# q and k of three attention heads projected early and parked in DRAM, with the order of TensorE and VectorE written out beside the top-k selection

## The chip, the cores and the metric

The kernel runs on one core of one Trainium2 chip. The metric is the device time of one execution in microseconds, as the median of the runs shown. The engines are called by their profile names: PE (TensorE matmul), PEld (its weight loads), DVE (VectorE), ACT (ScalarE), POOL (GpSimd) and SP (SyncE, which issues most transfers).

## The reference, cut to what matters

One transformer block over 1024 positions of width 1024, all in float32: a modulation vector, a sparse attention whose 256 keys per query are picked by an index score, a gated linear attention (GLA), a mix of the two, and a gated feed-forward part.

```python
mod = silu(c) @ w_mod + b_mod                 # six vectors: sh1, sc1, g1, sh2, sc2, g2
h = rms_norm(x, norm1_g) * (1 + sc1) + sh1
q, k, v, q_idx, k_idx, w_idx, gq, gk, gv, go, g_lr = split(h @ w_in)
score = einsum(relu(q_idx . k_idx), w_idx * idx_scale), causal      # 8 index heads of 64
sel = top_k(score, 256)                       # per query
att = softmax(q . k[sel] * att_scale) @ v[sel]                      # 4 heads of 128
gla = gla_chunked(gq, gk, gv, log_sigmoid(g_lr @ w_gate2 + b_gate2) / 16)   # 4 heads, dk 64, dv 128
mix = concat(rms_norm(att), rms_norm(gla) * silu(go)) @ w_out
x = x + g1 * mix
h2 = rms_norm(x, norm2_g) * (1 + sc2) + sh2
x = x + g2 * ((silu(gate) * up) @ w_down);  out = rms_norm(x, final_g)
```

## The kernel before

Every large product splits both factors into a rounded part and a rest and takes three matmuls for one (hi*hi, lo*hi, hi*lo). One projection of a 128-wide weight (`proj_T_plain`, `qk_proj`) runs as two units of 24 matmuls of 512 columns, a T unit each (lines L239 to L241). One of a 256-wide weight (`proj_N_plain`) runs as eight units of 24 matmuls of 256 columns, an N unit each (L248 to L250).

The work goes through these stages. First x is normed and transposed and the index projections are made; `scores(t)` then makes the index scores of query tiles 2 to 7 (PE L535 and L536, ACT L538, DVE L543). After that `units(jobs, ...)` walks a list of projection jobs: q, k and v of the two GLA pairs, the gates (`go`), v of the attention, and last q and k of the four attention heads. It is a generator with one step per unit, and each step is followed by `pump()`, which advances the background generators by the rates of `RATE`. These are `topk_act` ("ta": a bitwise search for the 256th score of tiles 7, 6 and 5, with three Sign passes per bit on ACT, L619, and four small operations on DVE, L621 to L626), `topk_dve` ("td": the same search for tiles 4, 3 and 2 with three counting passes on DVE, L590), and `gla_pair` (seven levels with POOL, ACT, DVE work in `prep` and eight PE matmuls in `level`, L757, whose result DVE takes with L762, and then eight chunks, L806 to L814). The loop ends when q and k of head 0 have begun and drains the selection.

The attention loop takes heads 0 to 3 and tiles 0 to 7. `att_step` makes the scores of one tile (L913 to L915), the transposes of the tile before (L930) and the values of the one before that (L939). Between these steps the remaining T units of q and k of heads 1 to 3 run (`next(main)`), `mods_late` makes the modulation vectors 2 to 5 (loads of `w_mod` on SP, DVE L657 and L659), and in head 3 `side` makes the GLA half of the mix (`mix_mm(t, 1, ...)`, L1011 to L1013). What is left of `side` runs behind the attention; then come the attention half of the mix, the second norm, the gate and up products (L1175 to L1177) and the down product (L1353 to L1355).

The Tile framework collects the instructions in the order in which they are traced, and orders each engine's queue itself by priority and readiness; `tc.high_priority` moves instructions forward in that order. Each engine then works through its own queue in order. Tiles of one tag share `bufs` slots, and a new tile waits for a free slot: `g` has 33 slots of 4 KB per partition, `gs` 4, `raw` 2, and the rings `whi` and `wlo` 4 each.

Of the kernel before, what the change touches and what calls it, by code (L numbers as in the profile page):

```python
# [41 lines left out]

RATE = {"ta": (0.8, 0), "td": (0.83, 2), "gla0": (1.1, 0), "gla1": (1.12, 0),
        "mods": (1.74, 0), "side": (0.41, -2)}
PRIORITY = {"td": 40, "side": 150, "mods": -40}
PROJ_FIRST = (1, 0, 1, 0, 1, 0, 1, 0)
PROJ = 0.5

# [4 lines left out]
W0_AT = 3  # L53
G1_AT = 2
OFF_BIAS = 1.0e30
# [10 lines left out]
def hymba_block_kernel(  # L66
# [32 lines left out]
    x1_d = dram.tile([L, D], F32, name="x1_d")  # L99
    hid_d = dram.tile([DFF, L], F32, name="hid_d")  # L100
    uid = [0]

# [224 lines left out]
    def proj_T_plain(w, dst, scale=None):  # L327
        for hf in range(2):
            pt = ps()
            chain_T(pt, w, slice(0, 128), *hT(hf), slice(0, 512))  # L330
            r = slice(hf * 512, hf * 512 + 512)
            if scale is None:
                A.copy(dst[:, r], pt)
            else:
                A.mul(dst[:, r], pt, scale)
            yield

# [9 lines left out]

    def pump():

        for name in list(bg):  # L350
            it, rate, due = bg[name]
            due += rate
            while due >= 1:
                due -= 1
                with tc.high_priority(PRIORITY[name]) if name in PRIORITY else nullcontext():
                    end = next(it, "end") == "end"
                if end:
                    del bg[name]
                    break
            else:  # L360
                bg[name] = (it, rate, due)
# [6 lines left out]
    def gate(p, w):  # L368
        drain(f"gla{p}")
        yield from gate_proj(p, w)  # L370

# [21 lines left out]
    def qk_proj(h, i, w):  # L393
        hi, lo = g([P, L], F32R), g([P, L], F32R)
        qk[h, i] = (hi, lo)
        for hf in range(2):
            pt = ps()
            chain_T(pt, w, slice(0, 128), *hT(hf), slice(0, 512))
            r = slice(hf * 512, hf * 512 + 512)
            A.copy(hi[:, r], pt)  # L400
            V.tensor_tensor(lo[:, r], pt, hi[:, r].bitcast(F32), ALU.subtract)
            yield

# [17 lines left out]
    for kind, p in (("go", 0), ("v", 0), ("v", 1), ("go", 1)):  # L421
        c0, fn = (C_GO, gate) if kind == "go" else (C_V, v_proj)
        le, he = low(len(jobs)), high(len(jobs))
        jobs.append((lambda c0=c0, p=p, le=le, he=he: wgroup256(w_in, c0 + p * 256, le, he), lambda w, fn=fn, p=p: fn(p, w)))
    for h in range(ATT_H):
        for i in range(2):
            jobs.append(job_qk(h, i))

# [117 lines left out]

    bias = {t: score[t].bitcast(BF16)[:, :(t + 1) * P] for t in score}
    bias[0], bias[1] = bias01[:, P:], bias01
    junk_d = cst.tile([P, 640], BF16, name="junk_d")
    top = {4: sc3[:, 512:832], 2: sc3[:, 832:1024], 3: sc5[:, 768:1024]}  # L550
    top = {t: top[t].bitcast(BF16) for t in top}
# [24 lines left out]
    def topk_dve(ts):  # L576
# [9 lines left out]
        for i in range(32):  # L586
# [10 lines left out]
            else:  # L597
                V.tensor_tensor(Z, m[:, :n], Z, ALU.bitwise_xor)
            yield
        for j, t in enumerate(ts):  # L600
            finish(t, Z[:, j:j + 1].bitcast(F32))
            yield

    def topk_act(ts):
# [9 lines left out]
        for i in range(32):  # L614
# [12 lines left out]
            else:  # L627
                V.tensor_tensor(Y, m[:, :n], Y, ALU.bitwise_xor)
            yield
        V.tensor_scalar(Y, Y, -2147483648, None, ALU.bitwise_xor)  # L630
        V.tensor_scalar(F, F, -2147483648, None, ALU.bitwise_xor)
# [14 lines left out]

    def mods_late():
        def acc_of(m, n):
            acc = g([P, 512], tag="h", bufs=4)
            for i in range(4):  # L650
                raw = g([P, 2, 512], tag="raw", bufs=NRAW)
                S.dma_start(raw, w_mod[2 * i * P:2 * (i + 1) * P, m * D + n * 512:m * D + (n + 1) * 512]
                            .rearrange("(k p) n -> p k n", p=P))
                for j in range(2):
                    cc = cs[:, 2 * i + j:2 * i + j + 1]
                    if i == 0 and j == 0:
                        V.tensor_scalar(acc, raw[:, j, :], cc, None, ALU.mult)  # L657
                    else:
                        V.scalar_tensor_tensor(acc, raw[:, j, :], cc, acc, ALU.mult, ALU.add)  # L659
                yield  # L660
            return acc

        def summed(m, n, acc):
            pt = ps()
            if m in (2, 5):
                T.matmul(pt[0:1, :], lhsT=ones[:, 0:1], rhs=acc, start=True, stop=True)
                row = g([1, 512], tag="h", bufs=4)
                A.copy(row, pt[0:1, :])
# [12 lines left out]

        last = None
        for m in (2, 3, 4, 5):
            for n in range(2):
                acc = yield from acc_of(m, n)
                if last is not None:
                    summed(*last)
                last = (m, n, acc)
        yield
        summed(*last)  # L690

# [139 lines left out]
    def gate_proj(p, w):  # L831
# [5 lines left out]
        for t in range(NT):  # L837
# [5 lines left out]
            if t % 4 == 3:  # L843
                S.dma_start(gla_d[(t - 3) * P:(t + 1) * P, p * 256:(p + 1) * 256].rearrange("(a p) d -> p a d", p=P),
                            sg[t // 4])
            yield

# [46 lines left out]
    bg["td"] = (topk_dve(SEL_D), *RATE["td"])  # L894
    while len(qk) < 2:
        next(main)
        pump()
    next(main)
    for name in list(bg):
# [6 lines left out]
    def att_scores(h, t):  # L906
# [10 lines left out]
        mx = small(1, tag="mx")  # L917
        V.tensor_tensor_reduce(sb[:, :W], pt[:, :W], bias[t], 1.0, NEG, ALU.add, ALU.max, mx)
        V.tensor_scalar(mx, mx, -att_scale, None, ALU.mult)
        z = small(1, tag="z")  # L920
        A.activation(sb[:, :W], sb[:, :W], AF.Exp, bias=mx, scale=att_scale, accum_out=z)
        return sb, z
# [12 lines left out]
    def att_values(h, t, pT, z):  # L935
# [5 lines left out]
        V.reciprocal(z, z)  # L941
        V.tensor_scalar(att[h // 2][t // 4][:, t % 4, hv], po[:, :P], z, None, ALU.mult)

# [81 lines left out]
    def side():  # L1025

        nxt = gla_pre(0)
        for t in range(NT):
            cur, nxt = nxt, gla_pre(t + 1) if t + 1 < NT else None
            mix_mm(t, 1, *cur)  # L1030
            if t % 2:
                wout_chunk(t // 2)
            yield

    bg["mods"] = (mods_late(), *RATE["mods"])
    proj = 0
    for h in range(ATT_H):
        if h % 2 == 0:
            att[h // 2] = [g([P, 4, 256]) for _ in range(2)]
        if h == G1_AT:  # L1040
            g1b = mod_bcast(0, 2 * D)
        if h == 3:
            for _ in main:
                pass
            drain("mods")
            for k in range(4, 8):
                wout_chunk(k)
            bg["side"] = (side(), *RATE["side"])
        for t in range(NT):
            att_step((h, t))  # L1050
            proj += PROJ if h else PROJ_FIRST[t]
            while proj >= 1:
                proj -= 1
                next(main, None)
            pump()
# [230 lines left out]
    for name in ("t3", "22", "t2", "t4"):  # L1286
        for _ in range(2):
            prepare()
        for qq, cols in late:
            row_sums((name,), qq, cols)  # L1290
    for s, k in order:
        if k == 0 and not s.up:
            sg = [g([P, L]) for _ in range(2)]
# [10 lines left out]


    g2b = mod_bcast(1, 5 * D)
    fin, acc = {}, {}
# [105 lines left out]
```

## Time and profile before

| what | value |
|---|---|
| median of 3 runs | 1442.97 us (1439.71 to 1443.05) |
| the profiled execution's own time | 1440.6 us |
| its span, first to last instruction | 1438.9 us |
| mean granted PE clock | 0.954 |
| busy: PE, PEld, DVE, ACT, POOL | 93%, 78%, 63%, 40%, 29% of the span |

The span is 1.7 us shorter than the execution's own time, and that time lies 2.4 us under the median. A busy share is an average over stages with different limits, and matmuls overlap, so the time of a PE matmul in the profile is its latency and not the distance to the next one. The granted clock is told as a share of full speed: 1.00 is 2.4 GHz and 0.50 is 1.2 GHz.

### The profile page before, as it was taken

What the parts mean: (1) busy time and instruction counts of PE and PEld (TensorE: products, weight loads), DVE (VectorE), ACT (ScalarE), POOL (GpSimd) and SP (SyncE); (2) the same over time, 40 slices, a digit from 0 to 9 for tenths busy, and PEclk for the clock granted to TensorE, in tenths of its full rate; (3) what the DMA queues carried; (4) which work ended last, traced back from release to release, by engine and by line L of the source; (5) the groups of instructions that cost most, each with busy time, mean ns of one, the idle gap of its engine ahead of it and who ended that gap; (6) DMA issues with size and microseconds to landing.
All of it is one profiled execution on the core that took longest, in us unless ns stands there. A gap on an engine that the chain in (4) does not pass through costs nothing.

```text
span 1438.9 us, 18354 instructions
## 1 busy us (share of the span) xinstructions
PE 1337.6 (93%) x6975; PEld 1121.2 (78%) x6975; DVE 899.8 (63%) x1577; ACT 571.7 (40%) x1026; POOL 423.7 (29%) x365
## 2 busy tenths in 40 slices
PE   5999946888899999999997999999999999999997
PEld 4777846677789888788886788888888887888886
DVE  3578999988737657665369644544444546575524
ACT  3466544665554233363176323233332335112202
POOL 3550621165100000023122334444433525223101
PEclk8999978999679999999999999999999999999999
DMA  9601001101001526552031222221222346264102
GB/s 266 200 15 44 16 0 30 30 13 47 30 17 44 177 74 186 179 215 78 30 136 40 88 88 76 86 83 66 86 88 79 97 146 212 100 201 146 45 15 103
DMA packets 93438, 132.16 MB, mean 92 GB/s; under 512 B 6211, under 2 KB 67746, under 8 KB 93350
## 3 DMA queue, kind: packets, MB, share of 16 engines
q1 hardware_dynamic: 93192, 130.93, 28.6%
q8 instruction: 55, 0.90, 0.3%
q14 instruction: 33, 0.27, 0.1%
q10 hardware_dynamic: 158, 0.06, 0.0%
HBM read 108.94 MB, written 22.03 MB: 91 GB/s over the span
## 4 chain that ended last, share of the span: by engine, by line
PE 64%; DVE 19%; DMA 5%; issue 4%; ACT 3%; SPq 2%; POOL 2%; ACTq 0%; DVEq 0%; POOLq 0%
PE pw L1175 4%; PE pw L1176 4%; PE pw L1177 4%; PE ps L1177 4%; PE ps L1175 4%; PE ps L1176 4%; DVE junk_d L590 4%; PE pw L1353 3%; PE ps L1353 3%; PE pw L1355 3%; PE ps L1355 3%; PE pw L1354 3%; PE ps L1354 3%; DMA raw<-in_w_mod_dram 2%; DVE h L745 2%
## 5 line engine op out<-in xcount | busy, mean ns | idle before, releaser
L619 ACT ACTIVATE junk_a<-g,Ya 128x1024 int8<-128x1024 f32 (+2 forms) x96 | 99.8, 1039 | 93.8 <-DVE Ya L626 92.8
L248 PE MATMUL ps<-whi,g 128*128 128x256 f32 x384 | 114.6, 298 | 0.0
L249 PE MATMUL ps<-whi,g 128*128 128x256 f32 x384 | 113.1, 294 | 0.0
L250 PE MATMUL ps<-wlo,g 128*128 128x256 f32 x384 | 113.0, 294 | 0.0
L1206 POOL TENSOR_TENSOR g<-g,h 128x512 f32<-128x512 f32 x33 | 51.9, 1572 | 138.0 <-DVE h L1218 74.1
L1319 POOL TENSOR_TENSOR raw<-raw,g 128x1024 f32<-128x1024 f32 x22 | 58.7, 2676 | 110.0 <-DMA raw<-in_w_down_dram 103.2
L239 PE MATMUL ps<-g,whi 128*128 128x512 f32 x208 | 84.1, 404 | 0.0
L241 PE MATMUL ps<-g,wlo 128*128 128x512 f32 x208 | 82.6, 397 | 0.0
L240 PE MATMUL ps<-g,whi 128*128 128x512 f32 x208 | 82.2, 395 | 0.0
L1177 PE MATMUL ps<-g,wlo 128*128 128x512 f32 x192 | 75.6, 394 | 6.3 <-DVE wlo L1168 6.2
L248 PEld LDWEIGHTS ps<-whi,g 128*128 128x128 f32 x384 | 78.1, 203 | 1.6 <-issue 1.4
L1175 PE MATMUL pw<-g,whi 128*128 128x512 f32 x192 | 76.9, 400 | 1.5 <-DVE h L1224 1.5
L249 PEld LDWEIGHTS ps<-whi,g 128*128 128x128 f32 x384 | 78.1, 203 | 0.0
L250 PEld LDWEIGHTS ps<-wlo,g 128*128 128x128 f32 x384 | 77.7, 202 | 0.2 <-issue 0.2
L1175 PE MATMUL ps<-g,wlo 128*128 128x512 f32 x192 | 75.4, 393 | 0.7 <-ACT g L1080 0.7
L1176 PE MATMUL ps<-g,wlo 128*128 128x512 f32 x192 | 75.3, 392 | 0.4 <-DVE g L1081 0.4
L1176 PE MATMUL pw<-g,whi 128*128 128x512 f32 x192 | 74.9, 390 | 0.0
L1177 PE MATMUL pw<-g,whi 128*128 128x512 f32 x192 | 74.8, 390 | 0.0
L956 POOL TENSOR_TENSOR raw<-raw,g 128x1024 f32<-128x1024 f32 x4 | 9.6, 2388 | 214.3 <-DMA raw<-in_w_out_dram 214.3
L590 DVE TENSOR_SCALAR_CACHE_REDUCE junk_d<-g,Zd 128x640 bf16<-128x640 f32 (+5 forms) x96 | 71.4, 744 | 1.8
L1168 DVE TENSOR_TENSOR whi<-gs,whi 128x512 fp32r<-128x512 f32 x44 | 37.8, 858 | 45.3 <-ACT whi L1167 44.7
L757 PE MATMUL pw<-h,gs 128*128 128x128 f32 x224 | 34.9, 316 | 30.5 <-DVE ma L622 16.4
(394 smaller groups left out, 3884.6 us busy)
## 6 DMA issues: line engine op xcount, KB each, us to landing
raw<-in_w_gate_up_dram SPq DMA_DIRECT2D x42, 512.0 KB, 3.5
raw<-in_w_mod_dram SPq DMA_DIRECT2D x32, 512.0 KB, 3.6
raw<-in_w_in_dram SPq DMA_DIRECT2D x24, 512.0 KB, 3.5
hid_d<-g SPq DMA_DIRECT2D x22, 512.0 KB, 3.0
raw<-in_w_down_dram SPq DMA_DIRECT2D x22, 512.0 KB, 3.4
gs<-hid_d SPq DMA_DIRECT2D x22, 512.0 KB, 3.3
g<-in_x_dram SPq DMA_DIRECT2D x16, 512.0 KB, 6.1
g<-in_w_mod_dram SPq DMA_DIRECT2D x16, 512.0 KB, 8.7
```

Of the source, the lines that this page charges most:

```text
L239: T.matmul(pt, lhsT=wh, rhs=rh, start=(k == 0), stop=False)
L248: T.matmul(pt, lhsT=rh, rhs=wh, start=(k == 0), stop=False)
L249: T.matmul(pt, lhsT=rl, rhs=wh, start=False, stop=False)
L250: T.matmul(pt, lhsT=rh, rhs=wl, start=False, stop=(k == KC - 1))
L590: V.tensor_scalar(junk_d[:, :W], top[t] if 0 < i < 16 else score[t], Z[:, j:j + 1].bitcast(F32), -float(TOPK), ALU.is_ge, ALU.add, accum_o ...
L619: A.activation(junk_a[:, :W], score[t], AF.Sign, bias=Y[:, j:j + 1].bitcast(F32), accum_out=acc[:, j:j + 1])
L1175: T.matmul(pt, lhsT=w[:, 0, kk, :], rhs=rh, start=(not more and kk == 0), stop=False, skip_group_check=more)
L1176: T.matmul(pt, lhsT=w[:, 0, kk, :], rhs=rl, start=False, stop=False, skip_group_check=more)
L1177: T.matmul(pt, lhsT=w[:, 1, kk, :], rhs=rh, start=False, stop=(kk == 3), skip_group_check=more)
L1353: T.matmul(po[m], lhsT=ah[:, r], rhs=wh[:, cc], start=(f == 0), stop=False)
L1354: T.matmul(po[m], lhsT=al[:, r], rhs=wh[:, cc], start=False, stop=False)
L1355: T.matmul(po[m], lhsT=ah[:, r], rhs=wl[:, cc], start=False, stop=(f == len(cur) - 1))
```

## The change

The projections of q and k of heads 1 to 3 become jobs among the GLA, gate and value jobs (`PARK_AT`). Each writes its result as float32 into a `g` tile, and SP stores it to the DRAM tile `qk_d`. In the attention, `qk_load(h)` reads both back one head ahead and splits them again into two parts. The rates are lower, a T unit counts as 1.87 steps and a step of the gate as 0.3. All units, q and k of head 0 included, now run before the attention, and `pin()` ties every PE and every DVE instruction of that loop to the one traced before it on the same engine, so that the order of both queues is the traced one. The selection writes its masks to tiles of its own (`bias_tiles`), not over the scores. The modulation vectors are spread: vector 2 during the last gate job, 3 and 4 during the attention, with loads issued by POOL into slots of the ring `whi`, and 5 in the feed-forward stage (`mod_g2`). `side` begins at head 0. The row maximum takes its scale in the reduction itself, which saves one small DVE operation (L919) per tile, and the division by the softmax sum (L942) moves from DVE to ACT.

```diff
-RATE = {"ta": (0.8, 0), "td": (0.83, 2), "gla0": (1.1, 0), "gla1": (1.12, 0),
-        "mods": (1.74, 0), "side": (0.41, -2)}
-PRIORITY = {"td": 40, "side": 150, "mods": -40}
-PROJ_FIRST = (1, 0, 1, 0, 1, 0, 1, 0)
-PROJ = 0.5
+RATE = {"ta": (0.46, 0), "td": (0.46, 1), "gla0": (0.58, 0), "gla1": (0.45, 0),
+        "mod2": (1.0, 0), "mods": (0.87, -1), "side": (0.33, 0.7)}
+LONG, SHORT = 1.87, 0.3
+PRIORITY = {"side": 150, "mods": -40}
+PARK_AT = (3, 6, 8, 10, 12, 14)
+QK_AT = 0
...
+    def qk_park(h, i, w):
+        st = g([P, L])
+        yield from proj_T_plain(w, st)
+        S.dma_start(qk_d[2 * (h - 1) + i], st)
+
+    def qk_load(h):
+        for i in range(2):
+            raw = g([P, L], tag="raw", bufs=NRAW)
+            S.dma_start(raw, qk_d[2 * (h - 1) + i])
+            hi, lo = g([P, L], F32R), g([P, L], F32R)
+            A.copy(hi, raw)
+            V.tensor_tensor(lo, raw, hi.bitcast(F32), ALU.subtract)
+            qk[h, i] = (hi, lo)
...
-    for h in range(ATT_H):
-        for i in range(2):
-            jobs.append(job_qk(h, i))
+    for at, job in zip(PARK_AT, parked):
+        jobs.insert(at, job)
+    jobs += [job_qk(0, i) for i in range(2)]
...
+    def bias_tiles(ts):
+        both = g([P, 2 * L], BF16)
...
-                raw = g([P, 2, 512], tag="raw", bufs=NRAW)
-                S.dma_start(raw, w_mod[...])
+                raw = g([P, 2, 512], tag=tag, bufs=NG if tag == "g" else NW)
+                (S if tag == "g" else G).dma_start(raw, w_mod[...])
...
-    while len(qk) < 2:
-        next(main)
-        pump()
-    next(main)
+    def pin():
+        traced = nc.cur_bb.bb.instructions
+        new = [i for i in traced[mark[0]:] if i.engine in (mybir.EngineType.PE, mybir.EngineType.DVE)]
+        for i in new:
+            if i.engine in before:
+                tc.add_manual_dep(i, before[i.engine].name, mybir.DependencyInfo(
+                    mybir.DependencyClass.NoSync, mybir.DependencyReason.DATA), reason="pin")
+            before[i.engine] = i
+        mark[0] = len(traced)
+
+    for steps in main:
+        pump(1 if steps is None else steps)
+        pin()
...
-        V.tensor_tensor_reduce(sb[:, :W], pt[:, :W], bias[t], 1.0, NEG, ALU.add, ALU.max, mx)
-        V.tensor_scalar(mx, mx, -att_scale, None, ALU.mult)
+        V.tensor_tensor_reduce(sb[:, :W], pt[:, :W], bias[t], -att_scale, -NEG, ALU.add, ALU.min, mx)
...
-        V.tensor_scalar(att[h // 2][t // 4][:, t % 4, hv], po[:, :P], z, None, ALU.mult)
+        A.activation(att[h // 2][t // 4][:, t % 4, hv], po[:, :P], AF.Copy, scale=z[:, 0:1])
...
-    bg["mods"] = (mods_late(), *RATE["mods"])
-    proj = 0
+    g1b = mod_bcast(0, 2 * D)
+    qk_load(1)
     for h in range(ATT_H):
...
-        if h == 3:
-            for _ in main:
-                pass
-            drain("mods")
-            for k in range(4, 8):
-                wout_chunk(k)
-            bg["side"] = (side(), *RATE["side"])
         for t in range(NT):
             att_step((h, t))
-            proj += PROJ if h else PROJ_FIRST[t]
-            while proj >= 1:
-                proj -= 1
-                next(main, None)
+            if h == 0 and t < 4:
+                wout_chunk(4 + t)
+                if t == 0:
+                    bg["side"] = (side(), *RATE["side"])
+                if t == 3:
+                    bg["mods"] = (mods_late((3, 4), ("whi",)), *RATE["mods"])
+            if h == ATT_H - 1 and t >= 4:
+                if t == 4:
+                    drain("mods")
+                wout_chunk(t - 4)
+            if t == QK_AT and 0 < h and h + 1 < ATT_H:
+                qk_load(h + 1)
             pump()
...
+    def mod_g2():            # vector 5: four loads of two halves, 32 DVE operations of 256 columns
...
+        if k in (1, 3, 5) and 2 <= s.pair.n < NF - 1:
+            next(mod5, None)
```

## Rows read from the trace of the kernel before

**Rows 1.** Stretches of the span: length, busy time (instructions) per engine, clock, DMA.

```profile
core 0: us, PE busy (x) PEld busy (x) DVE busy (x) ACT busy (x) POOL busy (x), PEclk, DMA share, GB/s
...
163.00:494.70 331.70, 279.27 (x1797) 252.64 (x1796) 261.24 (x652) 171.81 (x350) 86.26 (x60) 0.86 0.13 39
494.70:700.20 205.50, 200.16 (x1135) 169.41 (x1134) 124.54 (x288) 76.20 (x166) 22.93 (x36) 0.99 0.43 136
...
766.00:1190.00 424.00, 413.18 (x1799) 336.12 (x1798) 228.31 (x291) 138.08 (x227) 172.15 (x114) 0.99 0.27 88
```

**Rows 2.** Shorter stretches inside 163 to 494.7 us, same columns.

```profile
163.00:320.00 157.00, 116.09 (x723) 102.67 (x722) 148.16 (x398) 81.87 (x166) 55.84 (x41) 0.85 0.06 17
...
386.00:415.00 29.00, 29.00 (x110) 21.96 (x109) 10.46 (x44) 11.35 (x42) 1.68 (x2) 0.50 0.00 1
...
440.00:483.00 43.00, 43.00 (x322) 41.30 (x322) 35.40 (x73) 15.79 (x27) 0.00 (x0) 1.00 0.28 86
```

**Rows 3.** Waits of 133 to 490 us: total us, times, longest.

```profile
ACT junk_a L619 <- DVE Ya L626: 92.8, 26, 10.4
...
PE pw L757 <- DVE ma L622: 16.4, 1, 16.4
```

**Rows 4.** PE timeline: two GLA matmuls apart, ten matmuls of 256 columns, ten of 512.

```profile
376.77 0.49 PE L806 MATMUL pw<-g,g 128*128 128x128 f32 x2
377.02 0.36 PE L249 MATMUL ps<-whi,g 128*128 128x256 f32 x1
...
417.74 0.28 PE L248 MATMUL ps<-whi,g 128*128 128x256 f32 x1
...
418.94 0.28 PE L249 MATMUL ps<-whi,g 128*128 128x256 f32 x1
...
507.27 0.39 PE L239 MATMUL ps<-g,whi 128*128 128x512 f32 x1
...
509.54 0.39 PE L240 MATMUL ps<-g,whi 128*128 128x512 f32 x1
```

**Rows 5.** Line L240 on PE, PEld in two stretches, L659 on DVE in the first.

```profile
163.00:494.70 331.70, 26.01 (x65) 12.89 (x64) 0.86 0.13 39
494.70:700.20 205.50, 37.67 (x97) 18.07 (x96) 0.99 0.43 136
...
163.00:494.70 331.70, 7.49 (x10) 0.86 0.13 39
```

**Rows 6.** PE groups of 133 to 483 us: busy, mean ns, idle before them.

```profile
L757 PE MATMUL pw<-h,gs 128*128 128x128 f32 x224 | 34.9, 316 | 30.5 <-DVE ma L622 16.4 <-DVE h L745 8.0 <-DVE g L762 6.1
...
L809 PE MATMUL pw<-diag,g 64*128 64x128 f32 x56 | 19.1, 435 | 13.6 <-DVE diag L818 4.7 <-DVE diag L820 4.7 <-DVE Ya L626 4.1
L806 PE MATMUL pw<-g,g 128*128 128x128 f32 x64 | 18.9, 392 | 0.0
```

**Rows 7.** DVE groups: four of 494.7 to 700.2 us, the last of 163 to 494.7 us.

```profile
L659 DVE SCALAR_TENSOR_TENSOR h<-raw,cs,h 128x512 f32<-128x512 f32 x46 | 34.4, 748 | 12.2 <-DMA raw<-in_w_mod_dram 11.8
...
L942 DVE TENSOR_SCALAR g<-ps,z 128x128 f32<-128x128 f32 x32 | 11.1, 346 | 3.5 <-PE ps L939 3.2
...
L401 DVE TENSOR_TENSOR g<-ps,g 128x512 fp32r<-128x512 f32 x13 | 8.9, 685 | 4.2 <-ACT g L400 4.2
...
L919 DVE TENSOR_SCALAR mx<-mx 128x1 f32<-128x1 f32 x32 | 4.7, 145 | 0.1
...
L216 DVE TENSOR_TENSOR wlo<-raw,whi 128x1024 fp32r<-128x1024 f32 x11 | 13.8, 1258 | 2.0 <-ACT whi L215 1.8
```

**Rows 8.** PE timeline in head 3, idle time in brackets, and the stretch behind it.

```profile
629.27 0.33 PE L915 MATMUL pw<-g,g 128*128 128x384 f32 x1
632.37 0.50 PE L913 MATMUL pw<-g,g 128*128 128x512 f32 x1 [2.76 <-DVE mx L918]
...
634.00:638.00 4.00, 4.00 (x17) 3.47 (x16) 2.62 (x8) 3.54 (x11) 0.00 (x0) 0.57 1.03 411
```

**Rows 9.** DMA issues of 494.7 to 700.2 us: count, KB each, median us to landing.

```profile
raw<-in_w_mod_dram SPq DMA_DIRECT2D x25, 512.0 KB, 3.6
```

## What the change will do to the time

> **What bounds the kernel now.** The table says PE 93% busy, but that share is made of matmul latencies that overlap, so I read it by stage, with the busy time of the engines over the borders of the stages [rows 1]. Three stretches matter: the projections beside GLA and the top-k selection (163 to 494.7 us, 331.7 long, stage C from here on), the attention with the GLA half of the mix (494.7 to 700.2, 205.5 long), and the rest (738.7 to the end).
>
> In the attention the reader is to see PE busy for 200.2 of 205.5 us at a clock of 0.99: PE is the limit there, and every matmul taken out of it is worth its distance. In stage C the picture differs: 279.3 of 331.7 us at a mean clock of 0.86, with DVE at 261.2. It falls into parts [rows 2]. From 163 to 320 DVE is busy for 148.2 of 157 us, 94%, and PE for 116.1; from 440 to 483 PE is busy for all of 43.0 us and DVE for 35.4, 82%. In between lies a stretch from 386 to 415 in which PE never rests but runs at 0.50, 1.2 GHz, so that half of its 29 us are lost. The waits show why the two take turns [rows 3]: the Sign passes on ACT wait for the end of the step before on DVE for 92.8 us, and one wait of PE at a GLA level lasts 16.4 us, behind DVE's queue.
>
> How much of stage C is PE's own need? The timeline gives the distance of matmuls at full clock [rows 4]: ten of 256 columns in 1.20 us, so an N unit of 24 takes 2.88 us; ten of 512 columns in 2.27 us, so a T unit takes 5.45; and two of GLA's of 128 columns take 0.25. Line L240 is one of the three of a T unit: 65 in stage C are 8.1 units, 97 in the attention are 12.1 [rows 5]. So stage C needs 48 N units, 138 us; 8.1 T units, 44 us; and GLA's 344 instructions [rows 6] at 0.125, 43 us, with some 8 us for its short ones (an estimate). That is 233 us of 331.7: 99 us are waits and half clock.
>
> **The change, part by part.** *Twelve T units move.* Heads 1 to 3 have 3 x 2 x 2 = 12 units, 65 us. They leave a stretch that PE fills and go to one with 99 us of room. Stage C then needs 233 + 65 = 298 us of PE, and 302 with the sums of vector 2 and a spare 2 us (an estimate).
>
> *DVE in stage C.* A parked unit has no subtraction on DVE, only the copy on ACT, but its weights have one each: 6 x 1.26 = 7.6 us [rows 7]. Vector 2 brings 16 operations of 0.75, 12 us, in place of the ten (7.5 us) that run there now [rows 5]; and the matching weights and products of head 0 stay. Some 4 us of the selection that now lie before 163 come later (an estimate). So DVE goes from 261 to 277 us. ACT gets 12 copies and 6 casts, some 15 us (an estimate) on 172 of 332 us, which leaves it the least loaded of the three. Lower bound of the stage: 302 us if PE never waits; for DVE at the 94% of its densest stretch 295. Upper bound: none of the room is filled, 331.7 + 69 = 401. The rates are what decides. All units count 23 x 1.87 + 48 + 16 x 0.3 = 96 steps; 35 calls of each selection at 0.46 fill 76 of them, where they now run early (DVE at 94%) and leave PE alone at the end. The last 20 steps hold 8 N and 4 T units, 45 us of PE, and some 22 us of DVE (vector 2, half of the gate, weights), so about 255 us of either engine stand beside each other in the first 76. That both can run at once the stretch of 440 to 483 shows: PE full and DVE at 82%. I take that row: 277 / 0.82 = 338 us, 6 more than now, with PE at 89%.
>
> *The order.* `pin()` adds no semaphore between engines. What it takes away is the freedom to let a ready instruction pass a waiting one. Where DVE waits for the Sign passes at L621, the counting passes, the GLA products (L745) and the weight subtractions traced behind it wait too, and PE at its next GLA level for those. At 0.46 a step of the selection comes every 2.2 units, so the passes have some 7 us of other DVE work (255 / 76 x 2.2) before L621 asks for them. I cost the order inside the 338.
>
> *The attention.* 65 us of T units go. The row sums of vectors 2 and 5 go with them (some 4 us). What stays is 205.5 - 69 = 136 us of PE. DVE there falls from 124.5: L942 11.1, L919 4.7, twelve of L401 8.2, four weight subtractions 5, 14 of 46 vector operations 10 [rows 7], and gains six subtractions of `qk_load`, 7.5: 93 us. ACT, at 76, gains 32 divisions (0.35 each as on DVE, 11) and six casts and loses the casts of the twelve units and of their weights: some 80 (an estimate). Both hide behind PE. The filler is now `side` alone, 8 chunks over 24 steps. Where there is none now, in head 3 [rows 8], PE idles 2.76 us once and then runs at 0.57 for 4 us, about 4.5 us together. I take one such place more: 141 us; with none 136, with one in each head 154. The loads of q and k come a head early, and hh and hl, 16 slots of `g`, are free by then, so they hide; without that cover a head would begin later by a load and a split, some 6 us (an estimate from 3.6 [rows 9] and two operations of a microsecond and more).
>
> *The loads of vectors 3 and 4* now are issued by POOL, 16 of 512 KB, into the ring `whi`. From SP such a load lands in 3.6 us; the ring's four slots and some 24 steps of 4.4 us leave 6.6 us for each, so I cost them at nothing, and their cover is the 106 us until `wout_chunk(0)` needs the ring. The Trainium skill speaks against this part: the page "SBUF — State Buffer", section "Who interferes with whom", has it that POOL writes the descriptors of the transfers it issues and is locked out of the shared port while DVE runs an operation in a two-port mode. No row here shows a weight load issued by POOL. By the row the part adds 0; by the rule it would be the last rival below.
>
> *The feed-forward stage* gets vector 5: 32 DVE operations of 256 columns, some 13 us (an estimate from L659's 0.75 for 512), on a DVE busy for 228 of 424 us [rows 1]; PE's four sums take under 2 us, and their `ps` slot can hold up a product of the gate side four times. 3 us, bounds 0 and 12.
>
> *The sum:* 163 + 338 + 141 + 738.7 + 3 = 1383.7 us of span, against 1438.9; with 1.7 us around it 1385.4, beside the profiled execution's 1440.6. The median lies 2.4 us above that execution, so 1388.
>
> **The rivals.** *More is filled:* PE is never let wait, stage C takes 302 to 312 us. For it speaks that both needs come out even, against it that in none of these stretches both PE and DVE are over 90%. About 1350.
>
> *Nothing is filled:* the units add to stage C what they take from the attention, 401 us: 163 + 401 + 141 + 738.7 + 3 + 1.7 + 2.4 = 1451, or 1446 without the lost filler. The change then only carries work from one place to another. Against it speaks that T units need nothing from DVE and can lie in any gap of PE.
>
> *The fixed order costs more than it gives (slower):* in order, PE stands at a GLA step until DVE, itself in order, has come through the selection traced ahead. There are 14 levels and 16 chunks. From 390 us of stage C on the gain is gone, 52 us more than my 338, or 1.7 us at each of 30 places; the wait of 16.4 us [rows 3] and the 29 us at half clock [rows 2] behind a wait of 4.1 at L809 [rows 6] show how that could come together. With 3 us at each, stage C takes 428: 1478.
>
> *The attention starves (slower):* with the wait of 2.76 us [rows 8] at each of the 32 steps, 88 us, it ends at 1476; at a quarter of them, 1410, still faster. It decides from 20 steps on. Against it speak the 4 us behind that wait, in which PE is busy throughout.
>
> *The loads from POOL are late (slower):* at 12 us each, one after another, vectors 3 and 4 end 86 us late, `wout_chunk(0)` waits for the ring and the attention half of the mix for it: 1474; the point is 6.6 us each. That is the case that the page named above would give.
>
> **How the numbers follow.** I give my forecast (stage C 312 to 378 us) 0.77, more filled 0.07, nothing filled 0.06, the order slower 0.06, the starved attention 0.02, late loads 0.02. About 0.3%, 4.3 us, is what a measurement here can tell from no change. The bounds of the unknown costs around 1388 are stage C -26 and +40, the attention -5 and +13, the feed-forward -3 and +9; together by less than their sum, 1350 to 1434. Below lies some 0.06, above 0.13. Faster: forecast and more filled, 0.84; the same: half of nothing filled, 0.03; slower: the other half and the last three, 0.13.
>
> **What would show it.** In the profile of the changed kernel: stage C near 340 us with DVE at 80% and over, PE near 90% and the clock over 0.93 (right), or over 390 with PE waiting at L757 and L809 for DVE (the fixed order); L240 with no instruction in the attention and the attention with its mix near 140 us at a clock near 1.0, or short waits of the scores for L918 throughout; `w_mod` loads landing in under 6 us; and the gate and up stage at 424 us within 5. The prediction is wrong if the selection's steps on ACT, not DVE, set the pace (waits of DVE at L621 beyond 40 us), or if the slots of `g` run out in stage C and PE waits for an evacuation into a new tile.

## The result, and the profile after

The changed kernel takes 1429.15 us (median of four, 1428.47 to 1432.68), beside 1443.01 for the kernel before in the same comparison: a ratio of 0.9921, with a 95% interval of 0.9904 to 0.9938. It is 0.8% faster, clear of the noise, and inside the range, but it gained 14 us where 55 were forecast. One of the 51 runs of the kernel before took 1426.63 us, as did three of twelve (1426 to 1428) of the kernel before with two small edits, while all their others took 1438 us and more; why is open. First the page's head for the changed kernel, with the busy time of the span and the granted clock in 40 slices:

```profile
span 1426.8 us, 18366 instructions
...
PE 1323.9 (93%) x6979; PEld 1107.9 (78%) x6979; DVE 904.4 (63%) x1523; ACT 587.4 (41%) x1066; POOL 434.3 (30%) x381
...
PEclk9999989989999998998998999999999999999999
```

PE is still 93% busy, so the table shows nothing of the change. The stretches do. These answer to [rows 1]: stage C, the attention with its half of the mix, the rest, and the gate and up products (columns as there):

```profile
163.00:533.70 370.70, 321.62 (x2044) 285.34 (x2043) 278.49 (x672) 181.85 (x361) 82.55 (x60) 0.94 0.20 63
533.70:685.50 151.80, 138.71 (x847) 121.19 (x845) 91.77 (x192) 76.19 (x183) 31.17 (x45) 0.93 0.40 134
685.50:1426.80 741.30, 723.27 (x3190) 589.64 (x3188) 424.23 (x493) 237.58 (x388) 254.82 (x180) 0.99 0.31 103
...
751.00:1175.00 424.00, 415.83 (x1796) 335.47 (x1794) 245.67 (x320) 138.51 (x231) 171.79 (x113) 0.99 0.29 96
```

Against the forecast the rest is right to half a microsecond (741.3, where 738.7 + 3 stood; 738.7 is its length before, from 700.2 us on), the attention is 10.8 over (151.8 for 141), and stage C is 32.7 over (370.7 for 338). Those two are the whole miss. DVE's work is not it: 278.5 us in stage C (277 forecast) and 91.8 in the attention (93).

A stretch can be split in three: time in which PE is idle (length less PE busy), time that the half clock takes from a working PE (1 less the granted clock, times PE's busy time, added up over pieces of 4 us), and what is left, PE's own work at full clock.

| stage C | length | PE idle | lost to half clock | PE's own work |
|---|---|---|---|---|
| before | 331.7 | 52.4 | 35.1 | 244.2 |
| after | 370.7 | 49.1 | 13.0 | 308.6 |

PE's work grew by 64.4 us. Of these, 22.1 came out of the half clock and 3.3 out of the idle time; the other 39.0 made the stage longer. (44 of the 1152 matmuls of 256 columns, some 5 us at 0.12 each, now run before 163 us, so the units and the sums brought about 70 us in all.)

In the attention the same sum gives 67.7 us less work, but idle time went from 5.3 to 13.1 and the loss to the half clock from 1.6 to 7.8. Of these 20.9 us, 10.8 lie in its first 20 us and 7.8 between 641.7 and 657.7. In each of the two places PE waits for a load of GLA's output (`gla_d`, transposed at L1035), and the half clock follows:

```profile
541.12 1.11 PE L1035 MATMUL ps<-ident,g 128*128 128x128 f32 x4 [3.19 <-DMA g<-gla_d]
...
646.73 1.09 PE L1035 MATMUL ps<-ident,g 128*128 128x128 f32 x4 [2.22 <-DMA g<-gla_d]
```

```profile
541.70:545.70 4.00, 1.97 (x8) 1.28 (x6) 3.32 (x4) 2.51 (x5) 0.00 (x0) 0.50 0.34 98
...
649.70:653.70 4.00, 4.00 (x19) 3.90 (x20) 3.69 (x10) 0.69 (x3) 0.00 (x0) 0.50 0.25 101
```

Where PE stands in stage C the view of its waits tells (total us, times, longest); it answers to [rows 3], and the last line is ACT's wait there. After's L785 and L773 are before's L757 and L745; L821 is GLA's transposes, L837 a chunk, L698 the sums of vector 2, L656 the end of a step of the search.

```profile
PE pw L785 <- DVE h L773: 18.2, 6, 9.3
PE pw L821 <- POOL g L806: 15.5, 2, 7.8
PE pw L837 <- DVE diag L848: 6.9, 1, 6.9
PE ps L698 <- DVE g L691: 5.0, 1, 5.0
...
ACT junk_a L649 <- DVE Ya L656: 70.5, 28, 7.4
```

These four lines hold ten waits of PE, 45.6 of its 49.1 us of idle time. The first of them, in the timeline (start, us, engine, line; idle time in brackets):

```profile
174.90 1.22 DVE L219 TENSOR_TENSOR wlo<-raw,whi 128x1024 fp32r<-128x1024 f32 x1
...
176.73 0.88 DVE L619 TENSOR_SCALAR_CACHE_REDUCE junk_d<-g,Zd 128x640 bf16<-128x640 bf16 x1
...
180.54 0.16 DVE L651 TENSOR_TENSOR acca<-acca,need 128x3 f32<-128x3 f32 x1 [1.07 <-ACT junk_a L649]
...
181.21 0.87 DVE L619 TENSOR_SCALAR_CACHE_REDUCE junk_d<-g,Zd 128x640 bf16<-128x640 bf16 x1
...
183.86 1.73 DVE L773 TENSOR_TENSOR h<-g,gs 64x256 f32<-64x256 f32 x4
...
184.85 3.65 PE L785 MATMUL pw<-h,gs 128*128 128x128 f32 x16 [9.34 <-DVE h L773]
```

The reader is to see that DVE is not idle while PE stands: it goes through a weight subtraction, two counting steps of `topk_dve` (L619) and the ends of two steps of `topk_act` (L651, once waiting 1.07 us for ACT) before GLA's products (L773) have their turn. What they read was ready by 164.6 us (ACT's exponentials, L769), and PE's other factor by 167.8 (POOL, L778).

### The profile page after: what moved, and what is told of

The parts are those of the page before. It is cut to its first block, busy times and chain, and to the rows that moved or that the text cites. A ratio compares the mean times of both kernels' runs of the same rounds, so it can differ in the third digit from the quotient of the medians.

```text
span 1426.8 us, 18366 instructions
## 1 busy us (share of the span) xinstructions
PE 1323.9 (93%) x6979; PEld 1107.9 (78%) x6979; DVE 904.4 (63%) x1523; ACT 587.4 (41%) x1066; POOL 434.3 (30%) x381
## 4 chain that ended last, share of the span: by engine, by line
PE 67%; DVE 16%; issue 5%; ACT 4%; POOL 3%; SPq 2%; DMA 2%; ACTq 0%; POOLq 0%; DVEq 0%
PE pw L1212 4%; PE pw L1213 4%; PE pw L1214 4%; PE ps L1212 4%; PE ps L1214 4%; PE ps L1213 4%; PE pw L1418 3%; PE pw L1419 3%; PE pw L1420 3%; PE ps L1420 3%; PE ps L1419 3%; PE ps L1418 3%; DVE junk_d L619 2%; PE ps L242 2%; PE ps L978 2%
## 5 line engine op out<-in xcount | busy, mean ns | idle before, releaser
L649 ACT ACTIVATE junk_a<-g,Ya 128x1024 int8<-128x1024 f32 (+2 forms) x96 | 99.9, 1041 | 73.6 <-DVE Ya L656 70.5
L251 PE MATMUL ps<-whi,g 128*128 128x256 f32 x384 | 112.4, 293 | 2.4 <-DVE whi L216 2.1
L252 PE MATMUL ps<-whi,g 128*128 128x256 f32 x384 | 110.2, 287 | 0.0
L1384 POOL TENSOR_TENSOR raw<-raw,g 128x1024 f32<-128x1024 f32 x22 | 58.8, 2677 | 110.0 <-DMA raw<-in_w_down_dram 101.6
L251 PEld LDWEIGHTS ps<-whi,g 128*128 128x128 f32 x384 | 75.4, 196 | 7.4 <-issue 6.7
L252 PEld LDWEIGHTS ps<-whi,g 128*128 128x128 f32 x384 | 75.4, 196 | 0.1
L619 DVE TENSOR_SCALAR_CACHE_REDUCE junk_d<-g,Zd 128x640 bf16<-128x640 f32 (+5 forms) x96 | 71.4, 744 | 2.3
L1181 POOL TENSOR_TENSOR gs<-raw,raw 128x512 f32<-128x512 f32 x19 | 25.4, 1337 | 118.8 <-DMA raw<-in_w_gate_up_dram 94.0
L1205 DVE TENSOR_TENSOR wlo<-gs,wlo 128x512 fp32r<-128x512 f32 x44 | 39.4, 897 | 29.4 <-ACT wlo L1204 28.9
```

Of the source, the lines that this page charges most:

```text
L251: T.matmul(pt, lhsT=rh, rhs=wh, start=(k == 0), stop=False)
L252: T.matmul(pt, lhsT=rl, rhs=wh, start=False, stop=False)
L619: V.tensor_scalar(junk_d[:, :W], top[t] if 0 < i < 16 else score[t], Z[:, j:j + 1].bitcast(F32), -float(TOPK), ALU.is_ge, ALU.add, accum_o ...
L649: A.activation(junk_a[:, :W], score[t], AF.Sign, bias=Y[:, j:j + 1].bitcast(F32), accum_out=acc[:, j:j + 1])
```

## The experiments

Two theories stood at the start. Theory W: PE, in its fixed order, stands at a few places for results that come late, and moving these places gives the time back. Theory D: DVE's work with the search sets the length of the stage, and a wait taken away at one place comes back at the next. The kernel before had medians of 1439 to 1443 us in these comparisons.

**Without the fixed order** (the changed kernel, DVE's and PE's queues ordered freely):

```diff
     for steps in main:
         pump(1 if steps is None else steps)
-        pin()
```

> The changed kernel with no instruction of PE and DVE tied to the one before it; all else as changed. Theory W (waits at fixed places: stage C, 371 us long, has 46 us of PE waits at GLA steps, and the traced order keeps the moved units from filling them): free to let ready units pass, stage C loses 25 to 40 us and the time is 1390 to 1405. Rival D (DVE's own 278 us with the selection's chain set the length of stage C, in whatever order): 1425 to 1433. A third reading, that the fixed order is what made the moved units fill anything: 1440 or more.

Measured: 1437.37 us, ratio 0.9983 (0.9969 to 0.9997); stage C 382.3 us. This lies in none of the three ranges, nearest to the third. Freedom gives no gain, against theory W: the fixed order is worth 8 us of the 14. It does not shorten PE's idle time, which is 47.9 us without it and 49.1 with it. Without it stage C has 7.1 us more of half clock, and 43 more of the matmuls of 256 columns, some 5 us, which the changed kernel runs before 163 us.

**The fixed order alone** (`pin()`, as the change has it, in the loop of the kernel before):

```diff
...
     while len(qk) < 2:
         next(main)
         pump()
+        pin()
     next(main)
+    pin()
```

> The kernel before with only the fixed order added in its projection loop (PE and DVE in traced order, its own rates). Theory W: the order costs by itself, since GLA steps can no longer be passed: 1455 to 1475 against 1443. Rival D: DVE's work is the same, 1438 to 1448.

Measured: 1461.65 us, ratio 1.0164 (1.0138 to 1.0191), in theory W's range. Stage C and its three largest waits of PE:

```profile
163.00:523.00 360.00, 276.00 (x1752) 249.75 (x1752) 255.46 (x645) 171.97 (x344) 81.08 (x57) 0.81 0.11 31
...
PE pw L757 <- DVE h L745: 50.1, 9, 20.4
PE pw L809 <- DVE diag L820: 17.9, 7, 8.1
PE pw L793 <- POOL g L778: 15.7, 2, 10.2
```

PE is idle for 84 us (in the execution that was profiled, 1468.18 us, the longest of four). With the old list and the old rates the fixed order costs 1.6%, with the new ones it is worth 8 us: the rival that it costs more than it gives hangs on what is traced, and not on `pin()`.

**GLA's transposes two steps later:**

```diff
         level(*ahead)
+        yield
+        yield
         pt = pw()
```

> The changed kernel, with two more steps of the GLA generator between its products and the transposes (L821), so that units lie between. Theory W: the two waits of 7.8 and 7.7 us at L821 go, and some half clock behind them: 1410 to 1418. Rival D: the waits turn up elsewhere, 1425 to 1433.

Measured: 1416.75 us, ratio 0.9844 (0.9821 to 0.9867). PE's waits in stage C:

```profile
PE pw L785 <- DVE h L773: 18.8, 4, 9.3
PE pw L839 <- DVE diag L850: 16.0, 3, 6.5
PE pw L823 <- POOL g L806: 2.4, 1, 2.4
```

13.1 us of the wait for POOL go, 9.1 come back at the chunks, the wait at the sums of vector 2 falls from 5.0 to 0.4, and the idle time falls from 49.1 to 37.9 us. Theory W's number held, and part of what theory D said is in the second line.

**The six parked products all at the end of the list:**

```diff
-PARK_AT = (3, 6, 8, 10, 12, 14)
+PARK_AT = (10, 11, 12, 13, 14, 15)
```

> The changed kernel with the six parked jobs behind all others, before q and k of head 0, not spread. Theory W: spread, the twelve units (65 us) replaced about 25 us of half clock and no wait, so at the end they cost 25 to 35 us more: 1452 to 1466. Rival D (spread or not, they lie beside DVE's work): spread they would have been hidden, so all 65 us show at the end: 1480 to 1495. If spreading gave nothing: 1425 to 1435.

Measured: 1450.49 us, ratio 1.0075 (1.0059 to 1.0091). Stage C is 392.1 us, with 65.4 idle. The time is 1.5 us under theory W's range and far from theory D's. The same work in the same kernel, placed later, costs 21 us and more than the whole gain.

**Two more places moved** (with the transposes of above; the subtraction and the scans of the second pair's decays four units behind their activations, the loads of vector 2, and by the same code those of 3 and 4, one step ahead, with their sums a step later; cut):

```diff
         A.activation(la, la, AF.Ln, bias=1.0)
+        yield
         (G if p in DECAY_POOL else V).tensor_tensor(la, bT, la, ALU.subtract)
...
+            raws = [load(0)]
...
+                if i < 3:
+                    raws.append(load(i + 1))
```

> The changed kernel with the two units between a GLA level and its transposes of the run before, and two more places treated alike: the subtraction and the scans of the second pair's decays are traced four units after their activations, and each load of vector 2 one step ahead, with one step more before its sums. Theory W (the room in stage C is lost where PE, in its fixed order, stands at a few places for a result that is late by several microseconds): the waits of 6.9 us at the chunk behind the scans and of 5 us at the sums go, against 1416.8 with the GLA move alone: 1403 to 1410, stage C 349 to 356 us. Theory D (DVE's own work with its waits for the Sign passes sets the length, and a wait taken from PE comes back at the next level): 1414 to 1419, the waits of the levels for DVE longer by what is taken away.

Measured: 1404.69 us, ratio 0.9754 (0.9716 to 0.9792); stage C 350.6, idle 30.1; both lie in theory W's ranges. What PE still waits for:

```profile
PE pw L800 <- DVE h L788: 17.3, 4, 9.3
PE pw L854 <- DVE diag L865: 9.8, 2, 4.9
PE pw L838 <- POOL g L821: 2.4, 1, 2.4
```

L800 is after's L785, untouched.

**The mix's filler at a lower rate:**

```diff
-        "mod2": (1.0, 0), "mods": (0.87, -1), "side": (0.33, 0.7)}
+        "mod2": (1.0, 0), "mods": (0.87, -1), "side": (0.26, 0.7)}
```

> The changed kernel with the rate of the mix's GLA half in the attention at 0.26 in place of 0.33, so that its eight chunks last to the end of the attention. If the attention's 11 us over the forecast come from steps that have no filler (the clock falls behind the waits), 1423 to 1426. If they come from the waits at the start of a head, for loads and reciprocals, which lie where filler is traced too, 1428 to 1431.

Measured: 1421.27 us, ratio 0.9871 (0.9837 to 0.9905). The attention:

```profile
534.10:678.70 144.60, 133.61 (x847) 117.57 (x845) 94.73 (x192) 76.50 (x183) 30.59 (x45) 0.96 0.42 140
```

In the changed kernel the last chunk of the filler ran at 659 us and the attention went on to 685.5; here it lasts until 668 of 678.7. 7.2 of the 10.8 us come back, and the time is below both ranges: 4.3 of half clock and 2.1 of idle time, the rest in PE's work as split here.

But the steps without filler are not where they come from. In the changed kernel PE is idle for only 0.8 us between 659.7 and 685.5, at a clock of 1.00. What is gone is the place around 646.7 us. There SP issued the last load of `gla_d` at 642.73 us, and PE stood for it; here SP issues it at 631.57, and between 642.1 and 658.1 PE loses 1.0 us where it lost 7.8. The first 20 us of the attention lose 10.8 us in both kernels. So the place is the second reading's, a wait for a load where filler runs, but a lower rate does take it away.

**Vectors 3 and 4 loaded by SP:**

```diff
-                (S if tag == "g" else G).dma_start(raw, w_mod[...])
+                S.dma_start(raw, w_mod[...])
```

> The changed kernel with the loads of vectors 3 and 4 issued by SP, as in the kernel before, and not by POOL. The forecast had the place of issue at nothing: 1427 to 1431. If the loads from POOL are slowed by DVE and hold something up, 1418 to 1426. If SP's queue is the busier place, since the loads of q and k and of weights stand in it, 1432 to 1440.

Measured: 1429.0 us (median of nine), no difference from the changed kernel's 1429.15. The DMA lines of the page, first of the changed kernel, then of this one:

```profile
whi<-in_w_mod_dram POOLq DMA_DIRECT2D x16, 512.0 KB, 5.1
```

```profile
whi<-in_w_mod_dram SPq DMA_DIRECT2D x16, 512.0 KB, 4.9
```

**The attention's two small edits alone** (the kernel before with the scale inside the row maximum and the division on ACT):

```diff
-        V.tensor_scalar(mx, mx, -att_scale, None, ALU.mult)
...
-        V.tensor_scalar(att[h // 2][t // 4][:, t % 4, hv], po[:, :P], z, None, ALU.mult)
+        A.activation(att[h // 2][t // 4][:, t % 4, hv], po[:, :P], AF.Copy, scale=z[:, 0:1])
```

> The kernel before with only the two small edits of the attention: the softmax scale folded into the row maximum, which takes away a small DVE operation per tile, and the division by the sum on ACT. The forecast has DVE's relief there hidden behind PE: 1440 to 1446, no difference. If DVE's 15.8 us in the chain of scores, maximum and exponential did set the pace of that attention, 1428 to 1438. If the division on ACT, in order with the exponentials, is the later one, 1446 to 1452.

Measured: 1440.8 us, ratio 0.9984 (0.9953 to 1.0015). Nothing, as the forecast had it: PE covers both.

**The moved places and the lower rate together** (the edits of the two runs above in one kernel):

> The three moved places of the run before last (GLA's transposes two steps later, the second pair's decays in two parts, the loads of vector 2 a step ahead) together with the mix's GLA half at the rate 0.26. If the two effects lie in different stages, they add: stage C at 351 us, the attention at 144, the whole at 1404.7 - 7.5 = 1395 to 1399. If the filler's gain was borrowed from the start of the attention, 1400 to 1405.

Measured: 1398.64 us, ratio 0.9714 (0.9688 to 0.9740). The two effects add within the spread of the four runs (1396.51 to 1404.40): 6.0 us less than with the moved places alone, where the lower rate alone gave 7.9. This is the fastest kernel here with the whole computation, 30 us below the changed one.

**The same with GLA advanced ahead of the search:**

```diff
-        for name in list(bg):
+        for name in sorted(bg, key=lambda n: not n.startswith("gla")):
```

> As the run above, with GLA's generators advanced before the two selections after each unit, so that GLA's operations on DVE stand ahead of the selection's step traced at the same unit. The longest wait left, of TensorE at the chunks for the state on VectorE behind the selection's last masks (4.9 us twice and the half clock behind it), would go: 1384 to 1392 by theory W. Theory D: DVE then stands at GLA's products for ScalarE and GpSimd with nothing ahead of it, and the searches end later: 1396 to 1410.

Measured: 1403.44 us, ratio 0.9731 (0.9706 to 0.9756), in theory D's range; stage C is as long as without it (352.2), the idle time too (30.1 for 30.3). The wait at the first level falls from 9.34 to 4.86 us, but two waits of 4.9 and 4.6 at the chunks are now of 11.9 and 3.7. Theory D's reading holds for this change: it only moves the wait. The 4.8 us between the two medians do not show in these rows, since the profiled execution of the run above was its longest (1404.40).

**A quarter of the search** (8 of 32 steps of both searches, in the changed kernel; the masks then hold other keys), in `topk_act` and `topk_dve`:

```diff
-        for i in range(32):
+        for i in range(8):
```

> The changed kernel with 8 of the 32 steps of both searches, so that the masks hold other keys: it leaves out three quarters of the selection's search, some 130 us of DVE's work in stage C. It measures TensorE's own need there. If the need of 302 us is right and the waits for DVE are the rest, stage C falls to 312 to 328 us, with the waits for GpSimd and the decays left, and the time to 1370 to 1387. If TensorE needs more than the sum of units says, or other waits hold it, stage C stays over 345 us: 1404 and more.

Measured: 1415.65 us, ratio 0.9825 (0.9806 to 0.9844). The second reading's number, but neither for the reason that VectorE's load would be harmless nor for a larger need: another wait holds PE. Stage C, and that wait:

```profile
163.00:521.90 358.90, 318.19 (x2042) 284.19 (x2042) 193.51 (x384) 105.17 (x217) 86.04 (x60) 0.92 0.21 65
```

```profile
253.97 2.34 POOL L800 TENSOR_TENSOR gs<-g,g 128x1024 f32<-128x1024 f32 x1 [14.90 <-DVE g L603]
...
256.37 1.87 PE L809 MATMUL ps<-hsel,gs 128*128 128x2 f32 x8 [25.58 <-POOL gs L800]
```

85 us of DVE's work are gone (130 were expected to go), and PE is still idle for 40.7; its own work is 306.7. The search now ends at 206 us and the six masks (`finish`, L603 its last step) lie in one pile between 206 and 278; GLA's product on POOL waits for a `gs` slot behind them, and PE for POOL. The load had gone, but what was left of it stood in front of one GLA step.

**The same, spread:**

```diff
-RATE = {"ta": (0.46, 0), "td": (0.46, 1), ...
+RATE = {"ta": (0.15, 0), "td": (0.15, 1), ...
```

> As the run before, 8 of the 32 steps of both searches (so the masks hold other keys, and three quarters of the search are left out), but with the rates of both at 0.15 in place of 0.46, so that the eight steps and the six masks lie apart over the stage and not in one pile. TensorE's own work in stage C is 306 to 309 us in all runs with the twelve units; the rest is idle time and half clock. If VectorE's load sets the idle time, it falls from 49 to under 15 us: stage C 318 to 330, the time 1376 to 1388. If it is the lateness of a few results (GLA's first level, the transposes behind GpSimd, the decays, the sums behind their loads), 25 to 40 us stay: stage C 338 to 358, the time 1396 to 1416.

Measured: 1379.76 us, ratio 0.9589 (0.9569 to 0.9609), in the first reading's range. Stage C and PE's largest waits:

```profile
163.00:485.80 322.80, 311.59 (x2040) 278.58 (x2039) 202.85 (x383) 106.52 (x221) 86.20 (x60) 0.98 0.22 70
...
PE pw L821 <- POOL g L806: 6.4, 2, 6.0
PE pw L785 <- DVE h L773: 1.7, 1, 1.7
```

11.2 us idle, 5.1 lost to the half clock, 306.5 of work. The decays, the loads of vector 2 and GLA's chain over POOL and ACT are traced as in the changed kernel, and PE hardly waits at them. Between these last two runs the work is the same, and DVE is even busier here (202.9 us for 193.5): what separates 40.7 us of idle time from 11.2 is where the search and its masks are traced, above all how much of it together ahead of a GLA step.

## Why the prediction was wrong in size, step by step

*The step that failed* is the one that sized stage C: "That both can run at once the stretch of 440 to 483 shows: PE full and DVE at 82%. I take that row: 277 / 0.82 = 338 us". Its numerator was right; its divisor took a good stretch of 43 us for the rule of a stage, and one without a hand-over: between 440 and 483 POOL stands at 0.00 (x0) and PE runs projections alone (L239 to L241, L248 to L250), no GLA step. The other stretches of [rows 2] say the opposite: with DVE at 94% PE worked 116 of 157 us, and where PE never rested DVE did 10 of 29. The changed kernel still has these turns (columns as in [rows 1]):

```profile
203.00:243.00 40.00, 32.74 (x193) 28.71 (x192) 38.08 (x83) 20.96 (x37) 10.16 (x6) 0.96 0.18 53
243.00:283.00 40.00, 38.81 (x214) 31.36 (x214) 21.34 (x64) 21.25 (x45) 2.85 (x2) 0.96 0.18 54
283.00:323.00 40.00, 33.50 (x196) 29.59 (x197) 26.17 (x67) 24.68 (x53) 23.01 (x18) 0.87 0.10 27
...
363.00:403.00 40.00, 28.09 (x183) 25.89 (x182) 38.39 (x94) 20.36 (x36) 8.39 (x5) 0.88 0.30 92
403.00:443.00 40.00, 40.00 (x271) 35.15 (x271) 18.33 (x63) 22.46 (x54) 3.45 (x2) 1.00 0.13 40
443.00:483.00 40.00, 36.93 (x245) 32.50 (x244) 37.48 (x79) 5.54 (x24) 0.00 (x0) 1.00 0.05 14
```

In the two turns with DVE at 95 and 96% PE is idle for 7 and 12 us of 40; in the two with DVE near half, for 1 and none. A stage's average of 75% hides both. DVE's share alone does not decide it either: between 443 and 483 DVE is at 94% and PE idle for 3 us, none of them at a GLA step; between 283 and 323 DVE is at 65% and PE idle for 6.5, all of it in the wait at a chunk. The idle time of PE is not free room that any unit can fill: it lies at a few places, most of them GLA's steps, and a unit traced behind such a step stands behind it in PE's queue.

*The room.* "99 us are waits and half clock" was 87.5 by the split above, 52.4 and 35.1, because PE's own work was 244 and not 233. More weighs that the two were put together as one room. The units filled the half clock and left the idle time.

*PE's need after.* 302 us forecast, 306 to 309 in every run with the twelve units and the fixed order. The price of a T unit holds: about 70 us more work, 64.4 and the 5 before 163 us, against 65 for the units and 4 for the rest.

*The order at nothing.* "I cost the order inside the 338" was wrong in one way and right in another. The order itself is worth 8 us here. The "some 7 us of other DVE work" between the search's steps are a mean, meant as cover for L621, and ACT's wait for the search did fall, from 92.8 to 70.5 us. The sign that ACT would set the pace, waits of DVE for the Sign passes beyond 40 us, did not come: they are 17.2 us. But the search's steps themselves are what GLA's products stand behind in DVE's queue, and that side of the order had no price.

*The attention.* The forecast's 136 us hold the 6.9 us of idle time and half clock of before; the other 129.6 were PE's work, and 130.9 are found, so the work that moved out is priced well. "I take one such place more: 141 us" failed: idle time and half clock are 20.9 us, 14 more than before, where 4.5 were allowed, and they lie elsewhere. Where the filler has ended, PE is idle for 0.8 us. 18.6 us lie at the attention's start and around 646.7 us, mostly waits for the row maximum (L958) and for the loads of `gla_d`, and half clock behind them. Those loads have no term in the sum, and PE waits 5.4 us for them and then runs at half clock. The forecast's bound for one place without filler in each head (154) would have held, by luck: it was made for other places.

*DVE, ACT, the loads, the feed-forward.* DVE's 277 and 93 us measured 278.5 and 91.8. The loads of POOL cost nothing, though they took 5.1 us in the median (4.9 from SP) and not 3.6; the feed-forward's 424 us are the same, and the 3 us are 2.6 in the whole rest.

*The rivals.* "Nothing is filled" came nearer (stage C 401) than its chance of 0.06 says: 25 of 64 us were filled. "The fixed order costs more than it gives" has its mechanism in part: seven of the ten waits, 25.1 us, lie at the levels and chunks that it names, the others at GLA's transposes and the sums of vector 2. But the order gains 8 us here, so the rival itself is not what happened. The starved attention is there in small (5.6 us of waits for the row maximum, 3.6 before), and vectors 3 and 4 held nothing up.

What stays open: the runs with a quarter of the search also shorten the Sign passes, and with them ACT's work in stage C from 181.9 to 106.5 us, so the pace of DVE and of ACT are not told apart; and a spread of the whole search that leaves PE 11 us of idle time was not run. The way there in this kernel was the other one, to ask for the results later.

## What to carry to other kernels

Split the room of a stage into idle time and half clock before filling it: here extra work in the same queue won back 22.1 of 35.1 us of half clock, but idle time at a fixed place goes only if the work is traced ahead of that place or the late result is asked for later. For two engines that take turns, the load of the second matters by the stretch ahead of each hand-over, not by its average; two steps of distance in a generator gave 12 us, nearly as much as the whole change (14). The Trainium skill's page "Perfetto Trace Analysis", section "Optimization Strategy", says to find the gaps on the engine that matters and what blocks them, and to make those dependencies start sooner or finish faster; the traces here agree on the first half (ten gaps were 45.6 of 49.1 us), and show a third remedy, to put the consumer later.

## What the runs showed of the hardware

A load issued by POOL was no slower in effect than one by SP: 4.0, 5.1 and 7.2 us to landing (least, median and most of the sixteen) beside 3.8, 4.9 and 5.9 from SP in the run that changed only this, with DVE busy for 92 of the attention's 152 us, and the same time. The Trainium skill's page "SBUF — State Buffer", section "Who interferes with whom", would have POOL's descriptor writing locked out during DVE's two-port operations; no run here shows such a delay, and the trace does not tell which of DVE's operations ran in a two-port mode. One load, issued at 534.37 us, took 7.2 us, over the 6.6 that the forecast allowed; the DMA engines were 83% busy from 533.7 to 537.7 and 95% in the 4 us behind, and nothing waited for it.

The loss of granted clock outlasts a wait. Four stretches of the changed kernel, before, in and behind the wait of 6.9 us:

```profile
278.00:282.60 4.60, 4.59 (x35) 3.96 (x34) 2.35 (x8) 0.03 (x1) 2.21 (x1) 1.00 0.00 0
282.60:289.50 6.90, 0.00 (x1) 0.00 (x1) 6.66 (x15) 3.58 (x4) 6.47 (x7) 0.84 0.00 0
289.50:293.50 4.00, 4.00 (x15) 3.00 (x16) 1.32 (x5) 2.38 (x10) 3.00 (x3) 0.50 0.00 0
293.50:297.50 4.00, 4.00 (x21) 4.00 (x20) 2.57 (x9) 2.17 (x6) 1.28 (x1) 0.50 0.00 0
```

It falls inside the wait, and for 8 us behind it PE works without a rest at 0.50, the 1.2 GHz level. So this wait costs its 6.9 us and 4 more, half of those 8.
